# Scaling the decoded samples' delta-rule states: eight GpSimd operations in place of 64 on ScalarE

## The chip, the cores and the metric

The kernel runs on one core of one Trainium2 chip. Its time is the device time of one execution in microseconds (us). A core has several engines that work side by side, each through its own queue, in the order of that queue: TensorE (PE in the profile; PEld is its weight load) multiplies matrices, VectorE (DVE) and ScalarE (ACT) work on tensors in on-chip memory, GpSimd (POOL) is a slower, general one, and SyncE (SP) here only issues transfers (DMA). Matrix products go to a small memory of their own, PSUM; all other tiles lie in SBUF. 128 partitions are worked on at once, so "128x1024" is 1024 elements in each of 128 partitions.

## The reference, cut to what matters

One layer of a decoder trunk serves two groups of requests with the same weights: one prompt of 1024 tokens and 8 decoded samples of one token each. In the branch that the change touches, every sample carries for each of 8 heads a 128 x 128 state, and one token updates it:

```python
def _gdn_recurrent(q, k, v, beta, g, S0):
    def step(S, inp):
        q_t, k_t, v_t, b_t, g_t = inp
        S = S * jnp.exp(g_t)[..., None, None]
        delta = (v_t - jnp.einsum('bhk,bhkv->bhv', k_t, S)) * b_t[..., None]
        S = S + jnp.einsum('bhk,bhv->bhkv', k_t, delta)
        return S, jnp.einsum('bhk,bhkv->bhv', q_t, S)
...
y_a = _gdn_out(o_a, gdn_gate, lp['gdn_onorm_w']) @ lp['w_gdn_out']
y_b = o_b @ lp['w_swa_out']
mix = (jax.nn.sigmoid(ga) * y_a + jax.nn.sigmoid(gb) * y_b) @ lp['w_o']
```

The new state is the old one times a decay, plus the outer product of `k` and `delta`. Eight samples and eight heads make 64 such states; they are an output of the layer (`gdn_S_sample`). The output of the branch (`o`) is computed from dot products before the states are finished, so no later layer work reads the new states.

## The kernel before, in words

All 1032 tokens (1024 of the prompt, 8 samples) go through each projection together, in three parts of 384, 384 and 264 columns (part 0, 1 and 2; the samples are the last columns of part 2). A projection works tile by tile: for one output block of 128 rows (`j`) and one part, 24 matmuls run into one PSUM bank (8 blocks of the inner dimension by the three lines L180, L181, L182). There are three because every fp32 operand is split in a high and a low half: `split` copies the rounded value with ScalarE (L129) and subtracts it with VectorE (L130), and the product is high x high, high x low, low x high. So each weight tile is loaded by SyncE into a buffer `raw` (L135, 512 KB, one buffer: the next load waits until both halves of the last are made), becomes `wh` on ScalarE and `wl` on VectorE, and only then serves PE. The same holds for the activations: `load_part` (L1248) loads a part in four pieces of two blocks and splits each piece (`b2h`, `b2l`).

`branches` runs the two output projections one after the other: first `w_swa_out` over the attention's output, whose results VectorE multiplies by a gate (L1339), then `w_gdn_out` over the delta rule's output `oa`, in pairs of output blocks (`j0`, `j0 + 1`), whose results VectorE gates and adds (L1343, L1344). The gates come by SyncE too (L1391, `gt`).

Into the first of these, `sample_delta` is woven step by step (it is a generator; `branches` takes a step of it before each tile). Its last loop, over the heads, makes the new states. For each head `h`, SyncE loads `delta` of the 8 samples from `dlr` in main memory and repeats it over all 128 partitions (L1212, 512 KB) into `d`, which is one of two halves of a buffer, taken in turn (`h % 2`). Then `d` is multiplied by `k`, whose element varies with the partition and the sample (`kq`): for each sample one ScalarE operation of 128x128 (L1214) with that value as its scale. One VectorE operation per sample (L1215) multiplies the old state `S0[h]` by its decay (`egb`) and adds `d`. Last, GpSimd issues the store of the head's 8 states (L1217). A broadcast into a half of `d` has to wait until the head before last is through L1215.

The order of each engine's queue is not written out by hand: a scheduler with its own model of the times merges the steps of all streams into one queue for each engine, held only by the hints `issue_after` and by the dependences. Another operation or another duration in its model can therefore move work that the edit does not name.

Of the kernel before, what the change touches and what calls it, by code (L numbers as in the profile page):

```python
# [12 lines left out]
AF = mybir.ActivationFunctionType  # L13
ALU = mybir.AluOpType
# [4 lines left out]
P = 128  # L19
# [21 lines left out]
def bc(ap, dim, n):  # L41

    a = ap.unsqueeze(dim)
    shape = list(a.shape)
    shape[dim] = n
    return a.broadcast_to(shape)
# [18 lines left out]
class Step:  # L65
# [1053 lines left out]
    def sample_delta(self, pool2):  # L1119

        nc, I = self.nc, self.I
# [26 lines left out]
        kq = self.const([P, H, NS, 2], "kq")  # L1148
# [59 lines left out]
        for h in range(H):  # L1208
            if h % 4 == 0:
                yield  # L1210
            d = db[:, h % 2 * NP:h % 2 * NP + NP].rearrange("p (b v) -> p b v", b=NS)
            nc.sync.dma_start(d, dlr[h].unsqueeze(0).broadcast_to([P, NS, P]))  # L1212
            for b in range(NS):
                nc.scalar.activation(d[:, b, :], d[:, b, :], AF.Copy, scale=kq[:, h, b, 0:1])  # L1214
                nc.vector.scalar_tensor_tensor(S0[h][:, b, :], S0[h][:, b, :], self.egb[:, b, 0, h:h + 1], d[:, b, :],  # L1215
                                               op0=ALU.mult, op1=ALU.add)
            nc.gpsimd.dma_start(self.O[3][0][:, h].rearrange("b k v -> k b v"), S0[h])  # L1217
# [852 lines left out]
```

## Time and profile before

| what | value |
|---|---|
| median of 3 runs | 2089.26 us (2088.08 to 2090.94) |
| profiled execution, its own time | 2091.4 us |
| its span, first to last instruction | 2089.7 us |
| mean granted clock of TensorE | 0.986 |
| TensorE busy | 2022.6 us |
| VectorE, ScalarE, GpSimd busy | 1362.0, 901.3, 515.3 us |
| L1214 (the 64 scalings) | 64 operations of 384 to 405 ns, from 1186.9 to 1227.8 us |
| L1215 (the 64 updates) | 64 operations of 341 to 354 ns |
| L1217 (the 8 stores) | 0.89 us of GpSimd each to issue, 3.8 to 8.0 us to land |

The lines of the profile read like this. A line of the timeline is start, length, engine, line of the kernel, operation, output <- inputs (names without buffer numbers), form, count of merged instructions, and in brackets how long the engine had been idle before and what it had waited for; merged instructions overlap a little, so lengths add up to somewhat less than their sum. A line of the waits is "who <- whom: us in total, times, longest". A grouped line has, behind the bar, the busy time, the mean in ns, and idle time before such instructions with what ended it. `SPq` is SyncE's queue: there the length is that of the issue, not of the transfer.

### The profile page before, as it was taken

How to read it: one execution, taken by the hardware profiler on the slowest of the kernel's cores; microseconds unless marked ns; L12 is line 12 of the kernel's file. 1: busy time of each engine (PE TensorE's matmuls, PEld its weight loads, DVE VectorE, ACT ScalarE, POOL GpSimd, SP SyncE). 2: the span in 40 equal slices, each digit the busy share in tenths (PEclk: the TensorE clock that was granted, in tenths of full speed). 3: DMA queues.
4: the chain of work that ended last, by engine and by line, in shares of the span. 5: the costliest groups of instructions: out<-in, count | busy, mean ns of one | idle time of the engine just before them, and what ended most of it. 6: DMA issues, size and time to landing. Idle time of an engine off the chain costs nothing.

```text
span 2089.7 us, 41318 instructions
## 1 busy us (share of the span) xinstructions
PE 2022.6 (97%) x16245; PEld 1920.9 (92%) x16245; DVE 1362.0 (65%) x2734; ACT 901.3 (43%) x2233; POOL 515.3 (25%) x594
## 2 busy tenths in 40 slices
PE   7999999899999999989999999999999999999898
PEld 4987778799999999989988999999999999999898
DVE  4756767573746756556554575478876776768876
ACT  4665544434334343442442452345544544544533
POOL 2000000121321211211111000005566556445521
PEclk9999999999999999999999999999999999999999
DMA  8256443142331322312266774523233233487972
GB/s 291 71 144 209 136 165 115 60 131 58 78 89 53 86 62 59 91 37 60 63 189 194 250 230 122 155 67 97 88 106 113 87 97 102 130 296 262 310 241 86
DMA packets 301887, 275.75 MB, mean 132 GB/s; under 512 B 59730, under 2 KB 248111, under 8 KB 301676
## 3 DMA queue, kind: packets, MB, share of 16 engines
q1 hardware_dynamic: 295642, 252.14, 39.4%
q0 software_dynamic: 5552, 20.37, 2.8%
q8 instruction: 127, 2.08, 0.4%
q14 instruction: 68, 0.56, 0.1%
q10 hardware_dynamic: 498, 0.61, 0.1%
HBM read 212.93 MB, written 62.51 MB: 132 GB/s over the span
## 4 chain that ended last, share of the span: by engine, by line
PE 84%; DMA 6%; DVE 5%; ACT 3%; issue 1%; SPq 1%; POOL 0%; DVEq 0%; POOLq 0%; ACTq 0%
PE mm L180 18%; PE mm L181 18%; PE mm L182 18%; PE wv L180 3%; PE wv L182 3%; PE wv L181 3%; PE wy L182 2%; PE wy L180 2%; PE wy L181 2%; PE pv L652 1%; PE pt L190 1%; DMA raw<-in_w_swa_out_dram 1%; PE tp L190 1%; PE mm L264 1%; PE sc L614 1%
## 5 line engine op out<-in xcount | busy, mean ns | idle before, releaser
L180 PE MATMUL mm<-b1h,wh 128*128 128x384 f32 (+1 forms) x1520 | 498.0, 329 | 2.8 <-ACT gt L1292 1.6
L181 PE MATMUL mm<-b1l,wh 128*128 128x384 f32 (+1 forms) x1520 | 490.2, 323 | 0.0
L182 PE MATMUL mm<-b1h,wl 128*128 128x384 f32 (+1 forms) x1520 | 488.8, 324 | 0.0
L180 PEld LDWEIGHTS mm<-b1h,wh 128*128 128x128 f32 x1520 | 287.2, 189 | 14.4 <-issue 7.1
L182 PEld LDWEIGHTS mm<-b1h,wl 128*128 128x128 f32 x1520 | 286.5, 189 | 5.1 <-issue 4.5
L181 PEld LDWEIGHTS mm<-b1l,wh 128*128 128x128 f32 x1520 | 287.3, 189 | 4.0 <-issue 1.9
L129 ACT ACTIVATE wh<-raw 128x1024 fp32r<-128x1024 f32 x83 | 87.0, 1049 | 126.9 <-PE mm L181 73.7
L130 DVE TENSOR_TENSOR wl<-raw,wh 128x1024 fp32r<-128x1024 f32 x82 | 102.1, 1246 | 55.6 <-ACT wh L129 54.3
L181 PE MATMUL mm<-pk,w 128*128 128x260 f32 (+1 forms) x440 | 124.3, 283 | 1.1 <-DVE pk L130 1.1
L180 PE MATMUL mm<-pk,w 128*128 128x260 f32 (+1 forms) x440 | 124.5, 283 | 0.0
L182 PE MATMUL mm<-pk,w 128*128 128x260 f32 (+1 forms) x440 | 124.1, 282 | 0.0
L130 DVE TENSOR_TENSOR w<-ws,w 128x512 fp32r<-128x512 f32 x88 | 77.9, 887 | 36.6 <-ACT w L129 36.3
L1624 ACT COPY bml<-mm 128x256 f32<-128x256 f32 (+1 forms) x132 | 48.9, 371 | 97.9 <-PE mm L182 94.6
L182 PE MATMUL mm<-bmh,w 128*128 128x260 f32 (+1 forms) x320 | 90.2, 282 | 0.0
L180 PE MATMUL mm<-bmh,w 128*128 128x260 f32 (+1 forms) x320 | 89.9, 281 | 0.0
L1679 DVE SCALAR_TENSOR_TENSOR fa<-fz,fcw,fa 128x512 f32<-128x512 f32 x88 | 75.2, 873 | 18.4 <-ACT fa L1677 18.1
L180 PE MATMUL mm<-b2h,wh 128*128 128x384 f32 (+1 forms) x256 | 83.8, 330 | 2.9 <-ACT wh L129 2.9
L181 PE MATMUL mm<-b2l,wh 128*128 128x384 f32 (+1 forms) x256 | 84.2, 329 | 0.4 <-DVE b2l L130 0.4
L181 PEld LDWEIGHTS mm<-pk,w 128*128 128x128 f32 x440 | 82.8, 188 | 1.3 <-DVE pk L130 1.3
L182 PE MATMUL mm<-b2h,wl 128*128 128x384 f32 (+1 forms) x256 | 83.2, 327 | 0.0
L180 PEld LDWEIGHTS mm<-pk,w 128*128 128x128 f32 x440 | 82.9, 188 | 0.3 <-ACT bml L1624 0.2
L182 PEld LDWEIGHTS mm<-pk,w 128*128 128x128 f32 x440 | 82.9, 189 | 0.0
(649 smaller groups left out, 5914.2 us busy)
## 6 DMA issues: line engine op xcount, KB each, us to landing
raw<-in_w_in_dram SPq DMA_DIRECT2D x59, 512.0 KB
ws<-in_w_ffn_down_dram SPq DMA_DIRECT2D x55, 256.0 KB
raw<-xd SPq DMA_DIRECT2D x47, 258.0 KB
raw<-in_w_ffn_down_dram SPq DMA_DIRECT2D x47, 256.0 KB
raw<-in_w_ffn_gate_dram SPq DMA_DIRECT2D x22, 512.0 KB
raw<-in_w_ffn_up_dram SPq DMA_DIRECT2D x22, 512.0 KB
qst<-in_w_mod_dram SPq DMA_DIRECT2D x16, 512.0 KB
raw<-in_w_mod_dram SPq DMA_DIRECT2D x16, 512.0 KB
```

The source lines that it names most:

```text
L129: self.nc.scalar.activation(hi, x, AF.Copy)
L130: (eng or self.nc.vector).tensor_tensor(lo, x, hi.bitcast(F32), op=ALU.subtract)
L180: mm(ps, whi, xhi, start=first, stop=False, **kw)
L181: mm(ps, whi, xlo, start=False, stop=False, **kw)
L182: self.last_mm = mm(ps, wlo, xhi, start=False, stop=last, **kw).ins
L190: self.nc.tensor.transpose(out, in_, self.ident[:p, :p])
L264: nc.tensor.matmul(ps[32 * j:32 * j + 32], self.cT[:, k0 + j, :], ws[j // 2][:, j % 2, :], start=k0 == 0, stop=k0 > 0)
L614: self.scored = nc.tensor.matmul(sc[:, r, 256 - w:256], q, KH[:, lo:lo + w], start=True, stop=False)
L652: nc.tensor.matmul(pv[64 * r:64 * r + 64], V[:, n - back, ch], ps[:, r::2, :], start=back == 0, stop=back == (n > 0))
L1624: self.last_copy = nc.scalar.copy(r[p, i], x[p])
L1679: nc.vector.scalar_tensor_tensor(ai[:, c:e], zi[:, j + c:j + e], col(j), ai[:, c:e], op0=ALU.mult, op1=ALU.add)
```

## The change

For each head one GpSimd operation multiplies all of `d` (128x1024) by `kq`, repeated along the 128 columns of each sample. The eight ScalarE operations go.

```diff
             d = db[:, h % 2 * NP:h % 2 * NP + NP].rearrange("p (b v) -> p b v", b=NS)
             nc.sync.dma_start(d, dlr[h].unsqueeze(0).broadcast_to([P, NS, P]))
+            nc.gpsimd.tensor_tensor(d, d, bc(kq[:, h, :, 0], 2, P), op=ALU.mult)
             for b in range(NS):
-                nc.scalar.activation(d[:, b, :], d[:, b, :], AF.Copy, scale=kq[:, h, b, 0:1])
                 nc.vector.scalar_tensor_tensor(S0[h][:, b, :], S0[h][:, b, :], self.egb[:, b, 0, h:h + 1], d[:, b, :],
                                                op0=ALU.mult, op1=ALU.add)
```

The scheduler also orders other work anew. Three places show it.

SyncE's queue from the first `w_gdn_out` weight on, before (`b2l_2112` is part 2 of `oa`, `b2l_2114` its part 1, `b1l_2054` the buffer of `d`, `gt` the gates):

```order
L135 DMA raw_13486<-in_w_gdn_out_dram 128x8x128
L1248 DMA b2l_2112_13445<-oa_927 128x2x256 x2
L1391 DMA gt_13441<-sgb_2613 128x384
L1248 DMA b2l_2112_13445<-oa_927 128x2x256 x2
L1212 DMA b1l_2054_12756<-dlr_13111 128x1024
L1391 DMA gt_13523<-sga_2614 128x384
L1212 DMA b1l_2054_12756<-dlr_13111 128x1024
L135 DMA raw_13492<-in_w_gdn_out_dram 128x8x128
L1248 DMA b2l_2114_13461<-oa_927 128x2x384 x4
L1391 DMA gt_13556<-sga_2614 128x384
```

and with the change:

```order
L135 DMA raw_13430<-in_w_gdn_out_dram 128x8x128
L1248 DMA b2l_2112_13389<-oa_927 128x2x256
L1391 DMA gt_13385<-sgb_2613 128x384
L1248 DMA b2l_2112_13389<-oa_927 128x2x256 x3
L1212 DMA b1l_2054_12756<-dlr_13111 128x1024 x2
L1391 DMA gt_13467<-sga_2614 128x384
L1248 DMA b2l_2114_13405<-oa_927 128x2x384 x4
L135 DMA raw_13436<-in_w_gdn_out_dram 128x8x128
L1391 DMA gt_13500<-sga_2614 128x384
```

The second weight now stands behind the four loads of part 1, and these directly behind the third and fourth broadcast (heads 2 and 3).

PE's queue where the first `w_gdn_out` tile (output block 0, part 0) ends, before (`wh_13488` is the weight of block 0, `wh_13494` that of block 1; `b2h_2036` part 0, `b2h_2111` part 2 of `oa`):

```order
L182 MATMUL mm_13498<-b2h_2036_12688,wl_13489 128x384
L180 MATMUL mm_13531<-b2h_2036_12688,wh_13494 128x384
L181 MATMUL mm_13531<-b2l_2037_12689,wh_13494 128x384
L180 MATMUL mm_13564<-b2h_2111_13444,wh_13488 128x264
L181 MATMUL mm_13564<-b2l_2112_13445,wh_13488 128x264
```

and with the change (`wh_13432` is the weight of block 0, `b2h_2113` part 1 of `oa`):

```order
L182 MATMUL mm_13442<-b2h_2036_12688,wl_13433 128x384
L180 MATMUL mm_13574<-b2h_2113_13404,wh_13432 128x384
L181 MATMUL mm_13574<-b2l_2114_13405,wh_13432 128x384
L182 MATMUL mm_13574<-b2h_2113_13404,wl_13433 128x384
L180 MATMUL mm_13574<-b2h_2113_13404,wh_13432 128x384
```

Before, the first matmuls of block 1 and the tiles of part 2 came next; now it is the whole tile of block 0 over part 1, and the others follow it.

VectorE's queue in the same place, before (`b1h_1877` holds the states of heads 0 to 2, `b1l_1878` those of heads 3 to 5):

```order
L130 TENSOR_TENSOR b2l_2112_13445<-b2l_2112_13445,b2h_2111_13444 128x2x256 x3
L1339 TENSOR_TENSOR t_2041_12705<-mm_13316,gt_13341 128x384
L1215 SCALAR_TENSOR_TENSOR b1h_1877_11825<-b1h_1877_11825,egb,b1l_2054_12756 128x128 x8
L1215 SCALAR_TENSOR_TENSOR b1l_1878_11826<-b1l_1878_11826,egb,b1l_2054_12756 128x128
L1339 TENSOR_TENSOR t_2040_12704<-mm_13416,gt_13441 128x384
L1215 SCALAR_TENSOR_TENSOR b1l_1878_11826<-b1l_1878_11826,egb,b1l_2054_12756 128x128 x7
L130 TENSOR_TENSOR wl_13495<-raw_13492,wh_13494 128x1024
L1343 TENSOR_TENSOR gt_13523<-mm_13498,gt_13523 128x384
L130 TENSOR_TENSOR b2l_2114_13461<-b2l_2114_13461,b2h_2113_13460 128x768
L1344 TENSOR_TENSOR t_2040_12704<-t_2040_12704,gt_13523 128x384
```

and with the change:

```order
L130 TENSOR_TENSOR b2l_2112_13389<-b2l_2112_13389,b2h_2111_13388 128x2x256 x3
L1339 TENSOR_TENSOR t_2041_12705<-mm_13288,gt_13313 128x384
L1215 SCALAR_TENSOR_TENSOR b1h_1877_11825<-b1h_1877_11825,egb,b1l_2054_12756 128x128 x8
L1339 TENSOR_TENSOR t_2040_12704<-mm_13360,gt_13385 128x384
L1215 SCALAR_TENSOR_TENSOR b1l_1878_11826<-b1l_1878_11826,egb,b1l_2054_12756 128x128 x8
L130 TENSOR_TENSOR b2l_2114_13405<-b2l_2114_13405,b2h_2113_13404 128x768
L1343 TENSOR_TENSOR gt_13467<-mm_13442,gt_13467 128x384
L130 TENSOR_TENSOR b2l_2114_13405<-b2l_2114_13405,b2h_2113_13404 128x768
L1344 TENSOR_TENSOR t_2040_12704<-t_2040_12704,gt_13467 128x384
L130 TENSOR_TENSOR b2l_2114_13405<-b2l_2114_13405,b2h_2113_13404 128x768 x2
L130 TENSOR_TENSOR wl_13439<-raw_13436,wh_13438 128x1024
```

The splits of part 1 now come ahead of the second weight's `wl`; heads 2 and 3 stand ahead of both in either order. GpSimd's queue holds two of the new operations, then the stores of those two heads, in turn up to head 7.

## The prediction

> **What bounds the kernel now.** I read the page first, then the waits around the 64 scalings, the chain of waits there, and the timelines of the engines in it. The page's line of busy times (engine, busy us, share of the span, instructions):
>
> ```profile
> PE 2022.6 (97%) x16245; PEld 1920.9 (92%) x16245; DVE 1362.0 (65%) x2734; ACT 901.3 (43%) x2233; POOL 515.3 (25%) x594
> ```
>
> TensorE sets the end, so an edit counts only by the gaps it makes or closes on PE. ScalarE has 57% to spare in the mean; giving it less work is worth nothing unless it is the last to release PE somewhere. The view of waits for 1190 to 1215 us (who waited for whom: us, times, longest) has one such place:
>
> ```profile
> ACT b1l L1214 <- DMA b1l<-dlr: 6.7, 3, 3.2
> ...
> PE mm L180 <- ACT wh L129: 2.9, 1, 2.9
> ```
>
> and the chain of waits (start, length, what) leads to it over ScalarE's scalings:
>
> ```profile
> 1193.08 8.26 DMA b1l<-dlr
> ...
> 1201.43 0.41 ACT b1l L1214
> ...
> 1203.21 0.66 ACT b1l L1214 x2
> 1203.87 0.95 ACT wh L129
> 1204.83 0.04 issue
> 1204.87 0.69 PE mm L180
> ```
>
> PE needs the second `w_gdn_out` weight tile, ScalarE makes its high half `wh`, and ScalarE stood on the last of the L1214 operations until 1203.78. PE's timeline (start, length, instruction, idle before) shows the gap, the view by windows what came behind it (stretch, length, busy us of PE, PE's weight loads, DVE, ACT, POOL, then granted clock, DMA share, GB/s):
>
> ```profile
> 1197.68 0.34 PE L180 MATMUL mm<-b2h,wh 128*128 128x384 f32 x1
> ...
> 1198.03 0.34 PE L182 MATMUL mm<-b2h,wl 128*128 128x384 f32 x1
> ...
> 1201.67 0.34 PE L182 MATMUL mm<-b2h,wl 128*128 128x384 f32 x1
> 1204.87 0.69 PE L180 MATMUL mm<-b2h,wh 128*128 128x384 f32 x1 [2.86 <-ACT wh L129]
> ```
>
> ```profile
> 1205.00:1206.00 1.00, 1.00 (x4) 1.00 (x5) 1.00 (x2) 1.00 (x2) 0.70 (x1) 0.50 1.02 398
> 1210.00:1211.00 1.00, 1.00 (x7) 1.00 (x6) 0.48 (x1) 0.00 (x0) 0.00 (x0) 0.50 1.03 404
> 1211.00:1212.00 1.00, 1.00 (x8) 1.00 (x8) 0.00 (x0) 0.00 (x0) 0.00 (x0) 1.00 1.04 374
> ```
>
> After 2.86 us of idleness the clock stood at 0.50 until about 1211.0: 6.1 us at half speed lose another 3.05. So the stage already pays **5.9 us**, and that is all the change could gain here. At full clock a matmul of 384 columns comes every 0.173 us ((1201.67 - 1197.68) / 23), a tile of 24 takes 4.16.
>
> **What the change removes.** ScalarE's 64 scalings (grouped row: count, busy us, mean ns, idle before):
>
> ```profile
> L1214 ACT ACTIVATE b1l<-b1l,kq 128x128 f32<-128x128 f32 x64 | 19.4, 388 | 7.9 <-DMA b1l<-dlr 7.9
> ```
>
> 19.4 us busy. On the path lie at most the 0.7 us for which they delayed `wh` behind its weight tile (the chain's 0.66), and the clock's answer to the gap.
>
> **What it adds.** Eight GpSimd operations of 128x1024 with two inputs, on an engine that had only the stores of L1217 here. Each waits for its broadcast; behind it in GpSimd's queue stand only more of the same and the stores. None of this size is in the trace. The nearest rows, grouped by form:
>
> ```profile
> L1716 POOL TENSOR_TENSOR r<-fa,fa 128x256 f32<-128x256 f32 x33 | 27.9, 845 | 19.8 <-DVE fa L1701 19.8
> L1753 POOL TENSOR_TENSOR raw<-raw,ws 128x512 f32<-128x512 f32 x33 | 52.6, 1599 | 59.5 <-DMA ws<-in_w_ffn_down_dram 25.9 <-DMA raw<-xd 24.6 <-DMA raw<-in_w_ffn_down_dram 5.2
> ```
>
> Undisturbed ones took less (0.74 us for 256 and 1.30 for 512 columns, in the next fence): a line through these gives 1.30 + 2 x 0.56 = **2.4 us** for 1024. Lower end 2.0, if the broadcast second input comes cheaper; upper end 3.2, twice the mean of L1753. I take 2.4, since the disturbed rows contain waiting that I count separately. The Trainium skill, "GPSIMD Engine Reference", section 3.1, gives 4497 ns for a `tensor_tensor` of 2048 fp32 elements per partition and says to keep elementwise work on DVE; by it one operation would be an estimated 2.25 us and the sum below about 0.9 us less.
>
> Its length is not the worst of it. GpSimd and VectorE in the second half of the kernel, first GpSimd's timeline, then VectorE's:
>
> ```profile
> 1450.45 1.30 POOL L1587 TENSOR_TENSOR ws<-ws,raw 128x512 f32<-128x512 f32 x1
> 1451.70 0.74 POOL L1716 TENSOR_TENSOR r<-fa,fa 128x260 f32<-128x260 f32 x1
> 1452.40 0.74 POOL L1716 TENSOR_TENSOR r<-fa 128x260 f32<-128x260 f32 x1
> ```
>
> ```profile
> 1449.20 0.41 DVE L1701 TENSOR_TENSOR fa<-fa,mm 128x260 f32<-128x260 f32 x1
> 1450.58 2.85 DVE L1701 TENSOR_TENSOR fa<-fa,bml 128x260 f32<-128x260 f32 x1
> ```
>
> The same operation takes 0.41 us with one input in PSUM (`mm`) and 2.85 when both lie in SBUF and GpSimd began 0.13 us earlier: it ends 0.3 us after the third GpSimd operation in a row. The means say it too, over 33 and 22 instructions of one size:
>
> ```profile
> L1701 DVE TENSOR_TENSOR fa<-fa,bml 128x260 f32<-128x260 f32 x33 | 21.9, 663 | 0.7
> L1699 DVE TENSOR_TENSOR bml<-wv,bml 128x260 f32<-128x260 f32 x22 | 9.4, 425 | 3.5 <-ACT bml L1624 1.8 <-PE wv L182 1.5
> ```
>
> So the two engines take turns wherever VectorE reads two SBUF tensors. L1215, L130 (`wl`, `b2l`) and L1344 do; L1339 and L1343 (one input in PSUM) do not. The Trainium skill, "SBUF — State Buffer", section "Who interferes with whom", calls the port pair that both use an exclusive lock, held for the whole instruction; by that rule, which speaks against this change, eight operations take 8 x 2.4 = 19 us of port from the busiest helper of this stage. The 2.85 against 0.41 agrees.
>
> **Where that lands.** VectorE's timeline before, in the stretch that decides:
>
> ```profile
> 1186.10 1.23 DVE L130 TENSOR_TENSOR wl<-raw,wh 128x1024 fp32r<-128x1024 f32 x1 [4.39 <-ACT wh L129]
> ...
> 1189.98 2.18 DVE L1215 SCALAR_TENSOR_TENSOR b1h<-b1h,egb,b1l 128x128 f32<-128x128 f32 x8
> 1192.08 0.55 DVE L1339 TENSOR_TENSOR t<-mm,gt 128x384 f32<-128x384 f32 x1
> ...
> 1192.94 0.69 DVE L130 TENSOR_TENSOR b2l<-b2l,b2h 128x512 fp32r<-128x512 f32 x1
> 1193.60 1.23 DVE L130 TENSOR_TENSOR wl<-raw,wh 128x1024 fp32r<-128x1024 f32 x1
> 1194.75 1.89 DVE L130 TENSOR_TENSOR b2l<-b2l,b2h 128x512 fp32r<-128x512 f32 x3
> ...
> 1206.46 0.95 DVE L130 TENSOR_TENSOR b2l<-b2l,b2h 128x768 fp32r<-128x768 f32 x1
> ```
>
> Consecutive operations overlap by some 0.07, so I count 2.1 for a head's eight L1215, 0.47 for L1339 and L1343, 0.62 and 0.87 for a `b2l`, 1.15 for `wl`.
>
> Step 1. The first two GpSimd operations run back to back from 1187.3 (end of `wl`) to 1192.1. Behind them stand small ones 0.3, heads 0 and 1 (4.2), L1339 0.47, `b2l` 0.62, `wl` 1.15: the first `w_gdn_out` weight is whole at 1198.9. Before it was at 1194.8, and PE wants it at 1198.03. **PE waits 0.9.** What covered `wl` until now was 3.2 us of slack.
>
> Step 2. PE's new order has, right behind that tile (end 1202.75), the tile over the *second* part of `oa`, where the old order had others first. VectorE's queue puts heads 2 and 3 ahead of the split of that part: three `b2l` 1.8, two L1339 0.94, heads 2 and 3 4.2, the first `b2l` 0.87, and GpSimd's third and fourth operation 4.8, altogether 12.6: 1198.9 + 12.6 = 1211.5. The L1339 can hide under GpSimd (0.9 less); a late broadcast can add as much. PE starts at 1211.4. **Stall 8.65.**
>
> Step 3. The other three `b2l` (2.6), L1343 and L1344 (0.94) follow, and GpSimd's fifth and sixth operation may fall between them, 0 to 4.8. With both, the last quarter is there at 1219.9 and its six matmuls, at half clock, end at 1222.0; at full clock and without waits the tile would have ended at 1215.6. Extra 6.4, and 4.0 with one of the two between.
>
> Step 4. Half clock runs on into the next tiles: 1.0, less than the 3.05 above because step 3 has already counted most of it.
>
> The four tiles that follow are the same work in both. **Sum**: 0.9 + 8.65 + (4.0 to 6.4) + 1.0 = 14.5 to 16.9, less the 5.9 of the old stall: +8.6 to +11.0. I take **+10**. Heads 4 to 7 then run beside full tiles, and the stores of L1217 have no reader, so later delay costs nothing. The profiled execution took 2091.4 us (span 2089.7), 2.1 above the median; the difference is put on the median: 2089.3 + 10 = **2099.3 us**. With 2.0 in place of 2.4 the sum falls by 6 x 0.4 = 2.4, with 3.2 it rises by 4.8: +6 to +16.
>
> **Rivals.**
>
> *The stall only moves (turn-taking weak).* ScalarE and SyncE in the old run:
>
> ```profile
> 1204.72 1.56 ACT L129 ACTIVATE b2h<-b2l 128x768 fp32r<-128x768 f32 x2
> 1207.69 1.58 ACT L129 ACTIVATE b2h<-b2l 128x768 fp32r<-128x768 f32 x2 [1.41 <-DMA b2l<-oa]
> ```
>
> ```profile
> 1193.08 0.38 SPq L1212 DMA_DIRECT2D b1l<-dlr  x1
> 1194.86 0.38 SPq L135 DMA_DIRECT2D raw<-in_w_gdn_out_dram  x1
> 1195.33 4.54 SPq L1248 DMA_DIRECT2D b2l<-oa  x4
> ```
>
> The third quarter of that part landed at 1207.65 while transfers ran at about 400 GB/s (the windows above). The new SP order puts the weight's 512 KB behind these loads (1.3 us sooner) but holds them behind the fourth broadcast, which waits for head 1 on VectorE: about 1.2 us later without turn-taking. They land as before; ScalarE and VectorE add 0.8 and 0.9, the first quarter is ready near 1205.5, PE idles 3.6 us and loses 3 to the clock, 1 more to pacing: 7.6 against 5.9, **+1 to +3, 2091**. Against it: every pair of the kind shown above was delayed.
>
> *The stall goes.* ScalarE is free at 1194 and turns weight and `oa` the moment they land. If the first quarter were split by 1201.85 and each next one 1.04 later, PE would not stop: -5.9, **2083.4**. It decides at the landing of `oa`: needed by about 1200, but its first load was issued at 1195.33 before and, with head 1's wait, at 1197 or later now, and the broadcast of 1193.08 took 8.26 to land.
>
> *GpSimd is dearer (3.2 us, or broadcasts arrive late as well).* Six operations on the way add 4.8, the clock 1: +16, **2105**. L1753's mean speaks for it, the undisturbed 1.30 against.
>
> That the scalings stay on ScalarE is excluded: none of L1214 is left in its queue.
>
> **Chances.** Forecast 0.64, stall moves 0.14, stall goes 0.08, dearer 0.14. Within 0.2% (4.2 us, about what a measurement of this kernel can tell) falls the second: 0.13; faster 0.08; slower 0.79. The range goes from the middle of the second case to just above the fourth, 2090 to 2107; the forecast's own is 2095 to 2105.
>
> **What would show it.** Right: TENSOR_TENSOR of L1213 near 2.4 us; L1215 operations of several us where GpSimd stands ahead; PE idle for 7 to 10 us near 1203, released by VectorE's `b2l`, and a clock of 0.5 behind it. Wrong: L1215 and `wl` keep 0.35 and 1.23 beside running L1213; or PE's wait there is released by the DMA of `oa`; or there is none.

## The result, and the profile after

| | before | with the change | ratio, 95% interval |
|---|---|---|---|
| first comparison, 6 runs each | 2090.19 us | **2099.9 us** (2097.48 to 2106.34) | 1.0038 [1.0023, 1.0053] |
| repeat on another chip, 12 runs of the change, 35 of before | 2094.62 us | 2098.72 us | 1.0016 [1.0003, 1.003] |
| profiled execution (first comparison): its time, span, granted clock | 2091.4, 2089.7, 0.986 | 2100.54, 2098.8, 0.984 | |

The change makes the kernel slower in both. By the ratios that is +8 us [5, 11] in the first and +3.4 us [0.6, 6.3] in the repeat (the quotients of the two medians, 1.0046 and 1.0020, are a little higher). By its middle the second lies inside the 0.2% that the prediction called no change, the first beyond it. The line of busy times of the changed kernel:

```profile
PE 2026.3 (97%) x16245; PEld 1924.0 (92%) x16245; DVE 1373.0 (65%) x2734; ACT 883.7 (42%) x2169; POOL 538.4 (26%) x602
```

ScalarE lost 17.6 us of work, GpSimd got 23.1. VectorE has the same 2734 instructions as before and is busy 11.0 us longer. Of these, 5.3 are in two lines next to the new operations: L1215 went from 18.3 to 22.2 us in all and L1206 from 0.28 to 1.71. The rest lies in other lines and is not shown to be the change's; in the repeat's profile (e5 below) VectorE is busy only 5.9 us longer, 1367.9. The timelines of GpSimd and of VectorE around the new operations show most of these 5.3:

```profile
1191.58 3.77 POOL L1213 TENSOR_TENSOR b1l<-b1l,kq 128x1024 f32<-128x1024 f32 x2 [5.83 <-DMA b1l<-dlr]
...
1201.47 3.89 POOL L1213 TENSOR_TENSOR b1l<-b1l,kq 128x1024 f32<-128x1024 f32 x1 [0.70 <-DMA b1l<-dlr]
1206.14 1.90 POOL L1213 TENSOR_TENSOR b1l<-b1l,kq 128x1024 f32<-128x1024 f32 x1 [0.79 <-DMA b1l<-dlr]
...
1216.50 2.61 POOL L1213 TENSOR_TENSOR b1l<-b1l,kq 128x1024 f32<-128x1024 f32 x1 [3.51 <-DMA b1l<-dlr]
```

```profile
1190.00 1.23 DVE L130 TENSOR_TENSOR wl<-raw,wh 128x1024 fp32r<-128x1024 f32 x1 [3.98 <-ACT wh L129]
...
1191.86 1.71 DVE L1206 SCALAR_TENSOR_TENSOR osm<-b2h,onw,sgs 128x64 f32<-128x64 f32 x1
1193.52 3.82 DVE L1215 SCALAR_TENSOR_TENSOR b1h<-b1h,egb,b1l 128x128 f32<-128x128 f32 x8
...
1197.39 2.19 DVE L1215 SCALAR_TENSOR_TENSOR b1h<-b1h,egb,b1l 128x128 f32<-128x128 f32 x8
...
1200.57 1.22 DVE L130 TENSOR_TENSOR wl<-raw,wh 128x1024 fp32r<-128x1024 f32 x1
1201.70 1.89 DVE L130 TENSOR_TENSOR b2l<-b2l,b2h 128x512 fp32r<-128x512 f32 x3
...
1205.39 3.85 DVE L1215 SCALAR_TENSOR_TENSOR b1h<-b1h,egb,b1l 128x128 f32<-128x128 f32 x8 [1.33 <-POOL b1l L1213]
...
1209.63 2.18 DVE L1215 SCALAR_TENSOR_TENSOR b1l<-b1l,egb,b1l 128x128 f32<-128x128 f32 x8
1211.73 0.95 DVE L130 TENSOR_TENSOR b2l<-b2l,b2h 128x768 fp32r<-128x768 f32 x1
...
1214.40 1.82 DVE L130 TENSOR_TENSOR b2l<-b2l,b2h 128x768 fp32r<-128x768 f32 x2
```

A multiplication takes GpSimd 1.90 us. The operations of heads 0 and 2 on VectorE, each of which meets the next head's multiplication on GpSimd, take 3.82 and 3.85 us for eight instead of 2.18; heads 1 and 3, with no multiplication beside them, keep 2.19 and 2.18. L1206, of 64 columns, takes 1.71. In the trace, one of a slowed head's eight operations carries the whole delay (1.98 and 2.01 us). It also goes the other way: the third multiplication, which met VectorE's splits at 1201.70, took 3.89 and ended 1.77 us after the last of them, while the splits kept their 1.89.

PE's timeline, and the view by windows behind its stop (columns as before the change):

```profile
1205.24 0.34 PE L180 MATMUL mm<-b2h,wh 128*128 128x384 f32 x1
...
1209.89 0.44 PE L180 MATMUL mm<-b2h,wh 128*128 128x384 f32 x1 [3.97 <-ACT b2h L129]
...
1212.73 0.69 PE L181 MATMUL mm<-b2l,wh 128*128 128x384 f32 x1 [2.39 <-DVE b2l L130]
...
1219.23 0.34 PE L180 MATMUL mm<-b2h,wh 128*128 128x384 f32 x1
```

```profile
1213.00:1214.00 1.00, 1.00 (x4) 1.00 (x5) 1.00 (x3) 0.07 (x1) 0.00 (x0) 0.50 1.06 402
...
1217.00:1218.00 1.00, 1.00 (x4) 1.00 (x4) 0.35 (x1) 0.00 (x0) 1.00 (x1) 0.50 0.90 332
1218.00:1219.00 1.00, 1.00 (x7) 1.00 (x7) 0.00 (x0) 0.00 (x0) 1.00 (x1) 0.99 0.87 265
```

PE idles 6.36 us ahead of the first tile over part 1, where it idled 2.86 before. The first wait ends with ScalarE's half of the activations, the second with VectorE's. ScalarE had waited for the transfer (its timeline, the four pieces of part 1):

```profile
1209.00 0.84 ACT L129 ACTIVATE b2h<-b2l 128x768 fp32r<-128x768 f32 x1 [9.33 <-DMA b2l<-oa]
1210.16 2.79 ACT L129 ACTIVATE b2h<-b2l 128x768 fp32r<-128x768 f32 x3 [0.32 <-DMA b2l<-oa]
```

The tile's other 23 matmuls run from 1212.73 to 1219.23, 6.50 us; at full clock 23 x 0.173 = 3.99 us, so half clock costs 2.5.

**Two profiles are not to be laid on each other by their clocks.** The spans differ by 9.1 us, and 3.9 of that had arisen before any instruction that differs: the `wl` at 1190.00 stood at 1186.10 before, and up to it the queues of all engines hold the same instructions. No instruction of the change accounts for that, and in the other profiles here, with the same queues up to there, it starts anywhere from 1185.96 to 1191.51. So I compare a local length: from the first matmul of the first `w_gdn_out` tile to the first one of L1437, in the next projection, which waits 2.06 us for ScalarE in every profile here. It was 1295.57 - 1197.68 = 97.89 us before and is 1302.85 - 1201.34 = 101.51: **+3.6 us**. The idle and half-clock time at the stop makes 6.4 + 2.5 - 5.9 = 3.0 of these; the other 0.6 is in pieces below 0.3 us, one of them a wait of 0.15 for the first weight's `wl`.

There is a later piece. One matmul of the normalization that follows waits longer (PE's rows with a wait, in the changed kernel, then before):

```profile
1341.23 0.70 PE L1504 MATMUL nr<-dg,ones 128*128 128x256 f32 x2 [1.91 <-DVE dg L1503]
```

```profile
1334.24 0.70 PE L1504 MATMUL nr<-dg,ones 128*128 128x256 f32 x2 [0.65 <-DVE dg L1503]
```

That is +1.3 us. Together the trace shows some +5 us, inside both intervals above, though only at the lower end of the first.

### The profile page after: what moved, and what is told of

The parts are those of the page before. It is cut to its first block, busy times and chain, and to the rows that moved or that the text cites. A ratio compares the mean times of both kernels' runs of the same rounds, so it can differ in the third digit from the quotient of the medians.

```text
span 2098.8 us, 41253 instructions
## 1 busy us (share of the span) xinstructions
PE 2026.3 (97%) x16245; PEld 1924.0 (92%) x16245; DVE 1373.0 (65%) x2734; ACT 883.7 (42%) x2169; POOL 538.4 (26%) x602
## 4 chain that ended last, share of the span: by engine, by line
PE 79%; DMA 7%; DVE 7%; ACT 3%; issue 1%; POOL 1%; SPq 1%; DVEq 0%; POOLq 0%; ACTq 0%
PE mm L180 18%; PE mm L181 17%; PE mm L182 17%; PE wv L180 2%; PE wv L182 2%; PE wv L181 2%; DMA raw<-in_w_swa_out_dram 2%; PE pv L652 1%; DMA ws<-in_w_ffn_down_dram 1%; PE wy L180 1%; PE wy L182 1%; PE wy L181 1%; PE pt L190 1%; PE tp L190 1%; PE mm L264 1%
## 5 line engine op out<-in xcount | busy, mean ns | idle before, releaser
L180 PEld LDWEIGHTS mm<-b1h,wh 128*128 128x128 f32 x1520 | 287.6, 189 | 14.5 <-issue 7.1
L1679 DVE SCALAR_TENSOR_TENSOR fa<-fz,fcw,fa 128x512 f32<-128x512 f32 x88 | 73.4, 855 | 17.2 <-ACT fa L1677 16.9
```

The costliest lines, as they stand in the source:

```text
L180: mm(ps, whi, xhi, start=first, stop=False, **kw)
L1679: nc.vector.scalar_tensor_tensor(ai[:, c:e], zi[:, j + c:j + e], col(j), ai[:, c:e], op0=ALU.mult, op1=ALU.add)
```

## The experiments

Two theories stood against each other. **Turn-taking**: GpSimd's multiplications hold up VectorE, which delays the splits and, through the buffer of `d`, the transfers. **Order alone**: the new instruction made the scheduler build another order, with the tile over part 1 second on PE, and that part's data cannot be there in time, whoever multiplies. Each experiment is one of the two kernels with one edit. Times and ratios are against runs of the kernel before on the same chip; the local length is that of the experiment's one profile, with its distance from 97.89.

| run | median, before | ratio, 95% interval | local length |
|---|---|---|---|
| e1_vector | 2095.68, 2094.05 | 1.0007 [0.9995, 1.002] | 99.36 (+1.5) |
| e2_no_scaling | 2091.97, 2094.05 | 0.999 [0.9979, 1.0002] | 97.25 (-0.6) |
| e3_order_alone | 2097.74, 2094.05 | 1.001 [1.0, 1.002] | 99.83 (+1.9) |
| e4_memset | 2094.3, 2094.05 | 0.9995 [0.9985, 1.0005] | 98.53 (+0.6) |
| e5_change_again | 2098.72, 2094.62 | 1.0016 [1.0003, 1.003] | 101.78 (+3.9) |
| e6_memset_same_order | 2097.17, 2094.62 | 1.0009 [0.9996, 1.0021] | 98.48 (+0.6) |
| e7_defer_scalar | 2092.04, 2094.62 | 0.9991 [0.9976, 1.0005] | 99.70 (+1.8) |
| e8_defer_gpsimd | 2090.86, 2094.62 | 0.998 [0.9969, 0.9992] | 96.59 (-1.3) |
| e9_part2_second_scalar | 2089.67, 2093.73 | 0.9985 [0.9975, 0.9995] | 93.26 (-4.6) |
| e10_part2_second_gpsimd | 2101.86, 2093.73 | 1.0043 [1.0026, 1.006] | 104.42 (+6.5) |
| e11_part2_second_deferred | 2099.66, 2093.73 | 1.0035 [1.0021, 1.0048] | 103.33 (+5.4) |

### Who multiplies, and whether anyone does

**e1_vector**: the eight multiplications on VectorE itself.

```diff
-            nc.gpsimd.tensor_tensor(d, d, bc(kq[:, h, :, 0], 2, P), op=ALU.mult)
+            nc.vector.tensor_tensor(d, d, bc(kq[:, h, :, 0], 2, P), op=ALU.mult)
```

> The eight 128x1024 multiplications on VectorE in place of GpSimd. Theory A (GpSimd's operation keeps VectorE's two-input operations waiting for all of its 1.9 us): VectorE now pays about 1.2 us per operation itself instead of 1.9 of waiting, so four of them ahead of the first split of oa's part 1 cost 4.9 in place of 7.6: faster than the change, +2 to +6 us against the kernel before, PE's wait for b2l 1 to 3 us shorter than the change's 6.4. Theory B (only the new queue order costs): the order is nearly the change's (13 of 24 matmuls of the part-1 tile come first), so +7 to +10. Theory C (part of the change's cost arises ahead of the first changed instruction and differs by execution): the offset ahead of it, 3.4 us in the change's profile, lies anywhere from 0 to 4.

VectorE needs 1.22 us for what takes GpSimd 1.90, and even with the eight in its own queue the local length grows by less than half of the change's. In busy time VectorE is hardly better off with its helper: 1367.9 us here, 1373.0 and 1367.9 in the two profiles of the change. The order is near the change's but not the same (PE turns to block 1 after 13 of the tile's 24 matmuls), so the smaller loss is not shown to come from the engine alone.

**e2_no_scaling**: the line left out; the states then get `delta` without the factor `k`.

```diff
-            nc.gpsimd.tensor_tensor(d, d, bc(kq[:, h, :, 0], 2, P), op=ALU.mult)
```

> The scaling by k is left out altogether: no ScalarE and no GpSimd operation, the queue order of PE stays that of the kernel before. Theory A and B: ScalarE's scalings were worth no more than the 0.7 us by which they delayed the second weight's high half, the weight itself lands at 1203; PE's wait there 2.0 to 2.9 us, time -2 to +1 us. Rival (ScalarE was what PE waited for): the wait and the half clock behind it go, -6 us.

Nothing is left of the loss. A stop of 3.44 us for the second weight's `wh` remains, at the place of the old one and with PE's old order: there the old stall does not need the scalings at all.

```profile
1210.65 0.44 PE L180 MATMUL mm<-b2h,wh 128*128 128x384 f32 x1 [3.44 <-ACT wh L129]
```

So the multiplication, or the order that it brings, is the cause of the loss; this run doesn't tell which.

**e4_memset**: GpSimd writes a constant into `d` and reads nothing; the product is left out.

```diff
-            nc.gpsimd.tensor_tensor(d, d, bc(kq[:, h, :, 0], 2, P), op=ALU.mult)
+            nc.gpsimd.memset(d, 1.0)
```

> GpSimd only writes the 128x1024 buffer (a memset in place of the multiplication; the scaling by k is left out). If GpSimd's reading is what takes turns with VectorE: L1215 stays at 0.34 us and the splits at 0.65 and 1.23 while the memset runs, and the time is that of the run without scaling, -2 to +2 us. If any GpSimd work on SBUF does it: L1215 operations of 1 us and more beside the memset, +2 to +8.

PE's order is again the old one, not that of the change, so e4 separates less than it was meant to: it shows that an operation on GpSimd in this place, with the same waits around it, need not cost anything. It takes 0.95 us, and the five L1215 that run beside the second one take 1.40 us, what five of an undisturbed head take (2.19 / 8 x 5 = 1.37).

### Order alone, and the same order without GpSimd's reading

**e3_order_alone**: the old kernel, scalings on ScalarE, with the change's order of tiles on PE.

```diff
-            for ts in ((0,), (2,), (1,)) if j0 == 0 else ((0,), (1,), (2,)):
+            if j0 == 0:
+                for j, t in ((0, 0), (0, 1), (1, 0), (0, 2), (1, 2), (1, 1)):
+                    with self.tc.issue_after(self.last_mm):
+                        self.project(w[j], oa, ya_out, (t,))
+                continue
+            for ts in ((0,), (1,), (2,)):
```

> The kernel before with its 64 ScalarE scalings, but PE made to take the tile of part 1 right behind the first tile, as in the change. Theory A: PE waits for the landing of part 1 and its split, 4.5 to 5.5 us, but VectorE is not late otherwise: +1 to +4 us. Theory B (order alone): as the change, +7 to +10 us.

PE's rows with a wait in this stage:

```profile
1208.91 0.69 PE L180 MATMUL mm<-b2h,wh 128*128 128x384 f32 x1 [4.07 <-ACT b2h L129]
1210.77 0.69 PE L181 MATMUL mm<-b2l,wh 128*128 128x384 f32 x1 [1.17 <-DVE b2l L130]
```

The order alone makes the wait for part 1's first piece as long as in the change (4.07 and 3.97), with a shorter one for VectorE behind it, and half of the local loss. That spoke for the order as part of the cause. But here the scalings still sit in ScalarE's queue, ahead of that very piece (ScalarE ends the fourth head's scalings at 1207.17, then makes `wh`, then the piece), and SyncE issues the weight ahead of part 1. The same wait came from another cause, which only the next pair could tell.

**e5_change_again** is the change unmodified, and **e6_memset_same_order** has the loop over the tiles of e3 (its lines are shown there) and two writes of 0.95 us in place of each multiplication of 1.90; again the product is left out. In the traces the queues of PE, VectorE, ScalarE and SyncE hold the same instructions in both until the tile over part 1 is through.

```diff
-            nc.gpsimd.tensor_tensor(d, d, bc(kq[:, h, :, 0], 2, P), op=ALU.mult)
+            nc.gpsimd.memset(d, 1.0)
+            nc.gpsimd.memset(d, 1.0)
```

> The changed kernel once more, beside the others of this call, since single executions of one kernel spread over several us here and the profile of the kernel before was 3 us ahead of every other profile already at 1160 us, where all queues are still the same. Theory A: its own cost is what arises between 1180 and 1260 us (3.9 in the first profile) and 1 to 2 us behind it: +4 to +7 us. If the first comparison (+8, interval +5 to +11) is to be taken at its middle, +7 to +10.

> The change's order on PE, SyncE and VectorE in the decisive stretch, but GpSimd only writes: two memsets of the 128x1024 buffer (0.96 us each, 1.9 together, as long as the multiplication); the scaling by k is left out. Theory A (turn-taking on reading): VectorE's L1215, wl and b2l stay undisturbed, the first split of part 1 comes 2 to 4 us earlier than in the change, time as with the order alone, +1 to +3 us. Rival (the wait for GpSimd's 1.9 us, not what it does to VectorE meanwhile): as the change, +4 to +8.

PE's rows with a wait of e5:

```profile
1207.64 0.66 PE L180 MATMUL mm<-b2h,wh 128*128 128x384 f32 x1 [3.91 <-DVE t L1339]
1210.52 0.69 PE L181 MATMUL mm<-b2l,wh 128*128 128x384 f32 x1 [2.22 <-DVE b2l L130]
```

and of e6, with the start of its VectorE and GpSimd timelines (its lines from 1214 on count one higher):

```profile
1206.38 0.44 PE L180 MATMUL mm<-b2h,wh 128*128 128x384 f32 x1 [1.98 <-ACT b2h L129]
1208.30 0.69 PE L181 MATMUL mm<-b2l,wh 128*128 128x384 f32 x1 [1.48 <-DVE b2l L130]
```

```profile
1190.03 0.28 DVE L1206 SCALAR_TENSOR_TENSOR osm<-b2h,onw,sgs 128x64 f32<-128x64 f32 x1
...
1191.75 2.19 DVE L1216 SCALAR_TENSOR_TENSOR b1h<-b1h,egb,b1l 128x128 f32<-128x128 f32 x8 [1.44 <-POOL b1l L1214]
...
1193.99 2.19 DVE L1216 SCALAR_TENSOR_TENSOR b1h<-b1h,egb,b1l 128x128 f32<-128x128 f32 x8
```

```profile
1189.75 0.95 POOL L1213 MEMSET b1l<- 128x1024 f32 x1 [5.93 <-DMA b1l<-dlr]
1190.76 0.95 POOL L1214 MEMSET b1l<- 128x1024 f32 x1
1191.65 0.95 POOL L1213 MEMSET b1l<- 128x1024 f32 x1
1192.66 0.96 POOL L1214 MEMSET b1l<- 128x1024 f32 x1
```

The repeat shows the same stop as the change, 6.13 us. With writes that keep GpSimd busy as long (0.95 + 0.96, one after the other), L1206 is at 0.28 and the heads at 2.19, and PE idles 3.46 instead of 6.1 to 6.4; the local loss falls from 3.9 to 0.6. Of the 2.7 us of idleness that go, 0.7 are of the second wait, for VectorE's split, and 1.9 of the first. The first has two causes close together. In e5 it is VectorE's L1339, the next instruction behind the slowed head 2, that ends it; it reads a `mm` bank of PSUM, and the new tile needs one. ScalarE's piece had been ready 0.7 us earlier. In the first profile of the change, L1339 ended at 1209.71 and the piece at 1209.84, after its late landing. Why the landing is late SyncE's timeline tells. In e5:

```profile
1195.21 2.57 SPq L1212 DMA_DIRECT2D b1l<-dlr  x2
...
1198.86 3.85 SPq L1248 DMA_DIRECT2D b2l<-oa  x4
```

and in e6:

```profile
1194.00 2.57 SPq L1212 DMA_DIRECT2D b1l<-dlr  x2
...
1197.73 3.98 SPq L1249 DMA_DIRECT2D b2l<-oa  x4
```

The loads of part 1 stand behind the broadcasts of heads 2 and 3, and these wait until VectorE is through heads 0 and 1 and the buffer is free. Measured from the first `w_gdn_out` tile (1199.08 in e5, 1200.08 in e6), the loads start 0.22 us ahead of it in e5 and 2.35 ahead in e6: 2.1 us. So turn-taking delays both, the one directly and the other through the buffer. Whatever ends the first wait, PE can do only one matmul before the second, so VectorE's first split of part 1 ends the stop as a whole: it is done 11.4 us after the start of the first `w_gdn_out` tile in e5 and 8.2 in e6. Turn-taking is the greater part of the local loss, and the order by itself about 0.6 us. The runs agree in direction only: 1.0016 and 1.0009 have overlapping intervals, so the split rests on one trace of each. The repeat's +3.4 us lies just below the +4 to +7 that was expected.

The later wait at L1504 is another matter. It is there without turn-taking too:

```profile
1337.70 0.70 PE L1510 MATMUL nr<-dg,ones 128*128 128x256 f32 x2 [1.76 <-DVE dg L1509]
```

It is 1.37 in e3, with the scalings on ScalarE, and 0.68 and 0.37 in e2 and e4, which have PE's old order. So in these traces GpSimd's reading is not what makes it; it goes with the order, by a path that is open.

### Can the stop be taken away?

**e7_defer_scalar** and **e8_defer_gpsimd**: on the old kernel and on the change, all of `oa` and the first two `w_gdn_out` weights are issued before the loop over the heads, and the broadcasts from head 2 on are held behind the weights' loads.

```diff
-            nc.sync.dma_start(d, dlr[h].unsqueeze(0).broadcast_to([P, NS, P]))
+            with self.tc.issue_after(self.w_load.ins) if h >= 2 else nullcontext():
+                nc.sync.dma_start(d, dlr[h].unsqueeze(0).broadcast_to([P, NS, P]))
...
-                next(samples, None)
+                if getattr(self, "osm", None) is None:
+                    next(samples, None)
...
+        while getattr(self, "osm", None) is None:
+            next(samples)
+        oa[2] = self.load_part(pool2, self.oa, 2, last=self.osm)
+        oa[1] = self.load_part(pool2, self.oa, 1)
+        first_w = [self.load_w(I["w_gdn_out"][0][:, j * P:(j + 1) * P]) for j in (0, 1)]
         for _ in samples:
             pass
-        oa[2] = self.load_part(pool2, self.oa, 2, last=self.osm)
-        oa[1] = self.load_part(pool2, self.oa, 1)
...
-            w = [self.load_w(I["w_gdn_out"][0][:, j * P:(j + 1) * P]) for j in (j0, j0 + 1)]
+            w = first_w if j0 == 0 else [self.load_w(I["w_gdn_out"][0][:, j * P:(j + 1) * P]) for j in (j0, j0 + 1)]
```

> The kernel before with ScalarE's scalings, but the broadcasts of heads 2 to 7 queued behind the load of the second w_gdn_out weight. If the late landing of that weight is what the old 2.9 us stall is made of: it lands 2 to 4 us earlier, the stall and the half clock behind it go, -4 to -6 us. If heads 2 to 7 then stand in the way of later tiles: 0 or slower.

> The change with the same deferral: only heads 0 and 1 stand ahead of the splits of part 1. Theory A: with two multiplications and two heads less ahead of it, the first split of part 1 waits for its landing alone, PE's waits fall from 6.4 to 2 to 4 us: -2 to +2 us against the kernel before. Theory B or a cost of the multiplication elsewhere: as the change, +4 or more.

PE's waits in e7:

```profile
1206.25 0.44 PE L180 MATMUL mm<-b2h,wh 128*128 128x384 f32 x1 [0.27 <-ACT wh L129]
1229.21 0.69 PE L180 MATMUL mm<-b2h,wh 128*128 128x384 f32 x1 [4.32 <-ACT wh L129]
```

and in e8:

```profile
1203.93 0.44 PE L180 MATMUL mm<-b2h,wh 128*128 128x384 f32 x1 [1.50 <-ACT b2h L129]
1204.92 0.44 PE L181 MATMUL mm<-b2l,wh 128*128 128x384 f32 x1 [0.55 <-DVE b2l L130]
```

With ScalarE, the old stop is gone but for 0.27, and the scalings are only late somewhere else: they now stand ahead of the third weight's `wh`, and PE stops there, 4.32 us. So the -4 to -6 us do not come (0.9991, its interval reaching past 1). With GpSimd the stop shrinks to 2.05 us, and the kernel is faster than before, 0.998 [0.9969, 0.9992]: about 4 us, better than the -2 to +2 expected, and 7.9 us below the change (e5, on the same chip). ScalarE, empty of scalings, is what the change had to offer, and it seems worth something once the transfers no longer wait for the heads: the local lengths of e7 and e8 are 99.70 and 96.59, while the intervals of their ratios overlap.

**e9_part2_second_scalar**, **e10_part2_second_gpsimd**, **e11_part2_second_deferred**: the old kernel, the change and e8, each with the tile over part 2, whose data are there early, as the second.

```diff
-            for ts in ((0,), (2,), (1,)) if j0 == 0 else ((0,), (1,), (2,)):
+            if j0 == 0:
+                for j, t in ((0, 0), (0, 2), (1, 0), (1, 2), (0, 1), (1, 1)):
+                    with self.tc.issue_after(self.last_mm):
+                        self.project(w[j], oa, ya_out, (t,))
+                continue
+            for ts in ((0,), (1,), (2,)):
```

> The kernel before with one thing changed: PE takes the tile of block 0 over part 2 (24 matmuls of 264 columns, 2.9 us, operands long ready) as its second tile. If the old stall is the second weight's lateness by 2.9 us and nothing else, PE's wait falls from 2.86 to under 1 us, the half clock behind it goes, -3 to -6 us. If the stall only moves to the next tile: 0.

> The change with the same order of tiles. SyncE still loads the second weight behind part 1, and VectorE still splits part 1 behind heads 2 and 3 and makes the weight's low half behind that: the weight is whole at about 1213 us of the old time axis, PE wants it at 1205. Theory A: PE waits 5 to 8 us for the weight instead of the splits, +2 to +7 us, no cure. If the order of PE's tiles is the cause (theory B): as the part-2-second kernel with ScalarE, -3 to -6.

> GpSimd's scaling with heads 2 to 7 deferred (as in the deferred run with GpSimd) and PE's order as in the two runs above. There the weight was split at 1208 to 1210 us and PE would want it at 1205: a wait of 2 to 4 us, -3 to +1 us against the kernel before, not better than the deferral alone.

PE's longest waits in this stage of e9, e10 and e11 (of e11 also the second longest):

```profile
1205.71 0.44 PE L182 MATMUL mm<-b2h,wl 128*128 128x384 f32 x1 [0.64 <-DVE wl L130]
```

```profile
1216.56 0.69 PE L180 MATMUL mm<-b2h,wh 128*128 128x384 f32 x1 [6.68 <-ACT wh L129]
```

```profile
1213.37 0.69 PE L180 MATMUL mm<-b2h,wh 128*128 128x384 f32 x1 [4.19 <-ACT wh L129]
...
1235.00 0.44 PE L182 MATMUL mm<-b2h,wl 128*128 128x384 f32 x1 [2.06 <-DVE wl L130]
```

On the old kernel this order removes the stop but for 0.64 us: 0.9985 [0.9975, 0.9995], the other version that beats both kernels. On the change it makes things worse, 1.0043: +9 us, more than the +2 to +7 expected, with a wait of 6.68 that lies within the 5 to 8 expected. There SyncE's queue keeps the second weight behind part 1 and the broadcasts, and the tile that now comes third needs that weight. e11 missed its expectation of -3 to +1 us: 1.0035 is +7.3 us, so this order spoils what e8 had gained. Its second weight, too, is issued behind the loads of part 1 (PE waits 4.19 for it), and the third weight's `wl` stands behind a head's updates on VectorE (2.06 more). An order of tiles is only as good as the order of the transfers under it.

## Why the prediction was right or wrong

**Direction, place and mechanism were right.** The time went to PE's stop between the first and the second `w_gdn_out` tile, VectorE held up by GpSimd ends the last of its waits, and half clock follows. The old stall of 5.9 as what stood to be gained was about right too: e9, which removes it but for 0.64, is 4.6 us shorter in its local length and 3 by its ratio. The sum itself was too large: 14.5 to 16.9 us of loss at the stop was forecast, 0.15 + 6.36 + 2.5 = 9.0 is there, so +3 at the place and not +8.6 to +11. That the first comparison came out near 2099.3 all the same is luck in good part: the traces account for some +5, 1.3 of it at a place the forecast did not name, and the repeat says +3.4.

**Its own signs** came out mixed. PE's stop, the slow L1215 and the clock of 0.5 are there. The operation is at 1.90 and not near 2.4, and PE idles 6.36 and not 7 to 10. The first part of the wait follows the landing of `oa`, which stood among the signs of being wrong; VectorE's split still ends the stop, as forecast.

**The length of one operation** was put at 2.4 us, with 2.0 as the lower end. It is 1.90: the line through 256 and 512 columns lay too high. Whether that is because the broadcast second input comes cheaper is not shown, since no run has one of this size without. By the Trainium skill, "GPSIMD Engine Reference", section 3.1, the estimate was 2.25 us; the measurement decides.

**Step 1, PE waits 0.9 for the first weight: 0.15.** The two multiplications took 3.77 us and not 4.8, so `wl` ended at 1201.79. The tile's first matmul stands at 1201.34 and its third, the first to need `wl`, at 1201.84 instead of 1201.69: a wait of 0.15. The slack of 3.2 us was eaten almost exactly.

**Step 2, a stall of 8.65: the right place, 6.36 in size.** VectorE's queue did stand as forecast, heads 2 and 3 ahead of the split. But the third and fourth multiplication cost it 1.33 us of waiting and 3.85 - 2.18 = 1.7 us for head 2, and nothing for head 3: 3.0 where 4.8 was counted. And the first 3.97 us end with the landing of part 1, not with VectorE's split. The rival of the moving stall had named that landing; e5 and e6 show that half of this wait is turn-taking as well, by way of heads 0 and 1 and the buffer.

**Step 3, 4.0 to 6.4 more while the other splits come: this failed.** It had the fifth multiplication fall between the splits. Its row above starts at 1216.50, after VectorE's last split ended at 1216.22, because its broadcast had landed only then (3.51 us of waiting for the DMA). No further idle time came; only half clock, 2.5 us. The late broadcast is not the whole reason. In e5 the fifth multiplication did fall between the splits (GpSimd's row, then VectorE's), and there it was GpSimd that waited:

```profile
1212.70 4.20 POOL L1213 TENSOR_TENSOR b1l<-b1l,kq 128x1024 f32<-128x1024 f32 x1 [1.92 <-DMA b1l<-dlr]
```

```profile
1212.19 1.82 DVE L130 TENSOR_TENSOR b2l<-b2l,b2h 128x768 fp32r<-128x768 f32 x2
1213.92 1.21 DVE L130 TENSOR_TENSOR wl<-raw,wh 128x1024 fp32r<-128x1024 f32 x1
```

The splits kept the length that they have in the change (1.82), and the multiplication ended 1.77 us after `wl`. What the step had wrong is who waits: VectorE, running without a gap, lost nothing.

**Step 4, 1.0 of half clock in the next tiles: none.** The window from 1218 is at 0.99, before that tile ends.

**What was missed** is the +1.3 us at L1504, over 130 us later. In e5 that wait is 2.02 as well. No run isolated it, but e6, which has no turn-taking, shows 1.76. The forecast had later delay cost nothing.

**The rivals.** The forecast kept the stall's move at +1 to +3 for the case of weak turn-taking; e6 is that case, with +0.6 locally and +1.9 us by its ratio, whose interval reaches below 1. That the stall goes was right about its worth but not about the change: it needs the transfers moved as well (e8) or the tiles (e9). The dearer GpSimd, +16, fell with the 1.90.

The Trainium skill, "SBUF — State Buffer", section "Who interferes with whom", says that a VectorE instruction with two SBUF inputs contends with a GpSimd instruction that reads SBUF, and not with one that only writes it. The pair agrees: L1206 takes 1.71 us beside the multiplication and 0.28 in e6 beside a write into the buffer of `d`.

## What to carry to other kernels

Work that is moved to GpSimd can be paid by VectorE wherever VectorE reads two operands in SBUF, and a small instruction can pay most of a GpSimd operation (1.71 us in place of 0.28); count that first along the queue of VectorE, and then along every transfer that waits for a buffer VectorE frees. A chain in which every operation is counted in full, each in the worst spot, comes out too long: here the engine that was already running did not wait, and a multiplication that met VectorE in a run of splits waited itself. And where a scheduler sets the order, look at what has moved on the transfer queue before reordering the compute: the same order of tiles gave 0.9985 over one transfer order and 1.0043 over the other.

## What the runs showed of the hardware that was not expected

- Turn-taking goes both ways: GpSimd's multiplication of 1.90 us took 3.89 beside VectorE's splits, in e5 3.62 and 4.20. Each of these ended 1.77 us after the last of VectorE's operations that ran without a gap, so GpSimd waited for the whole run of them and not for one.
- A GpSimd write of 128x1024 takes 0.95 us, half of the multiplication, and leaves VectorE's two-input instructions alone.
- Executions differ by several us in the middle of the kernel with the same instructions up to there: the `wl` ahead of the first GpSimd multiplication, up to which all queues are the same, started between 1185.96 and 1191.51 in the 13 profiles here. What sets this wasn't tried; it is why single spans here say little below some 5 us.
- Half clock need not begin when PE resumes. In the change it stands from the end of the stop; in e8, after idling 1.50 and 0.55 us, matmuls of 384 columns came every 0.173 us until 1206.07, 1.2 us after the second wait, and only then every 0.32 us, until 1209.50.
